# ifftshift of an 8192 x 8192 matrix: the order in which DMA packets walk the rows

## The chip, the cores and the metric

The kernel runs on one core of a Trainium2 chip. The metric is the device time of one execution in microseconds, median of several runs. Before the change it is 810.61 us (three runs, 810.15 to 810.87).

## The reference

```python
def setup_inputs():
    return {
        "x": np.random.randn(8192, 8192).astype(np.float32),
    }

def reference(x: np.ndarray) -> np.ndarray:
    return np.fft.ifftshift(x)
```

Both sides are even, so `ifftshift` moves every row by 4096 places and every column by 4096 places, around the end: `out[r, c] = x[(r + 4096) % 8192, (c + 4096) % 8192]`. The four quadrants change places diagonally. Nothing is computed; 268.4 MB (256 MiB) are read and as many are written.

## The kernel before

The kernel copies straight from the input in DRAM to the output in DRAM. No data comes into on-chip memory, and no compute engine has work. All DMAs are issued by SP (`nc.sync`), one after the other.

A row has 8192 floats, 32 KB; half a row, `hc`, is 16 KB, and a `piece` is half of that, 2048 floats or 8 KB. The function `both` (lines 25 to 34) issues one DMA for 64 rows (`rows = ENGINES * apart`, 16 x 4), and in each row for one piece of the left half and the same piece of the right half. The access pattern has three dimensions, outermost first: 64 rows with a step of one row, two halves with a step of half a row, 2048 contiguous floats. On the side of the input the halves go in the opposite order (step `-hc`) and the rows start 4096 further on, around the end. One DMA moves 64 x 2 x 8 KB = 1 MB.

The outermost dimension is split over the 16 DMA engines, so that each engine gets four neighbouring rows: engine e has rows 4e to 4e + 3 of the 64. Its eight packets of 8 KB are, in order, (row 0, left), (row 0, right), (row 1, left) and so on to (row 3, right). This order is not written in the loop; it follows from the access pattern.

The loops (lines 40 to 42) go over 128 blocks of 64 rows and, inside, over the two pieces of a half (`col`): 256 DMAs. Two successive DMAs thus finish a block of 64 rows, which is 2 MB of the input and 2 MB of the output, and the next two go on behind it.

The order of the work is that of the loops. The framework gives DMAs in turn one of eight semaphores, and from the ninth on each waits for the completion of the DMA eight places before it. So there are at most eight DMAs, 8 MB, in flight, and each DMA engine has up to eight DMAs' worth of packets queued.

Of the kernel before, what the change touches and what calls it, by code (L numbers as in the profile page):

```python
# [1 line left out]

# [4 lines left out]


ENGINES = 16  # L10


@with_exitstack
def kernel(
    ctx: ExitStack,
    tc: tile.TileContext,
    x: bass.AP,
    out: bass.AP,
):
    nc = tc.nc  # L20
    R, C = x.shape
    hr = R // 2
    hc = C // 2

    def both(queue, row, col, rows, piece):

        queue.dma_start(
            out=bass.AP(out.tensor, out.offset + row * C + col, [[C, rows], [hc, 2], [1, piece]]),
            in_=bass.AP(
                x.tensor,  # L30
                x.offset + (row + hr) % R * C + hc + col,
                [[C, rows], [-hc, 2], [1, piece]],
            ),
        )


    apart = 4
    piece = hc // 2
    rows = ENGINES * apart
    for row in range(0, R, rows):  # L40
        for col in (0, piece):
            both(nc.sync, row, col, rows, piece)


# [1 line left out]
_INS = ['x']  # L46
_OUTS = [((8192, 8192), 'float32')]


def kernel(**inputs):  # L50
    import numpy as _np
    import concourse.bacc as _bacc
    import concourse.tile as _tile
    from concourse import mybir as _mybir
    from concourse.bass_utils import run_bass_kernel_spmd as _run

    nc = _bacc.Bacc("TRN2", target_bir_lowering=False, num_devices=1)  # L57
    arrays, args = {}, []
    for name in _INS:
        a = _np.ascontiguousarray(inputs[name])  # L60
        if a.dtype.kind in "iu":
            a = a.astype(_np.int64)
        arrays[f"in_{name}_dram"] = a
        args.append(nc.dram_tensor(f"in_{name}_dram", a.shape, _mybir.dt.from_np(a.dtype), kind="ExternalInput").ap())
    for i, (shape, dtype) in enumerate(_OUTS):
        dt = _mybir.dt.from_np(_np.dtype(dtype))
        args.append(nc.dram_tensor(f"out_{i}_dram", shape, dt, kind="ExternalOutput").ap())
    with _tile.TileContext(nc) as tc:
        kernel(tc, *args)
    r = _run(nc, [arrays], core_ids=[0])  # L70
    got = tuple(r.results[0][f"out_{i}_dram"] for i in range(len(_OUTS)))
    return got[0]
```

## Time and profile before

| What | Value |
|---|---|
| median of the runs | 810.61 us |
| profiled execution, its own time | 810.44 us |
| its span, first to last instruction | 808.7 us |
| DMAs, size of each | 256, 1024 KB |
| packets on the DMA queue | 36864 |
| of these with data (8192 B) | 32768 |
| mean rate, one way | 332 GB/s |
| HBM read and written together | 664 GB/s over the span |
| median from issue to landing | 25.1 us |

The page shows only what an engine does for itself: here only four small constants that the framework writes with POOL, 0.2 us. What counts is the DMA part. The row "DMA" gives, in 40 equal slices of the span, the busy share of the 16 DMA engines in tenths; the row "GB/s" gives what they moved in each slice, one way (each byte is read and written once). "Busy" is from a packet's start to its end, whatever the packet waits for in between. The waits of SP's own queue ("SPq") tell whether the issuing of DMAs holds the DMA engines up. Line 27 is the `dma_start`, line 68 the end of the program.

The trace also has one record for each packet, with its start, its duration and its size, but without the engine's number; and the time of each of the 4096 completion signals, 16 for each DMA.

### The profile page before, as it was taken

What the parts mean: (1) busy time and instruction counts of PE and PEld (TensorE: products, weight loads), DVE (VectorE), ACT (ScalarE), POOL (GpSimd) and SP (SyncE); (2) the same over time, 40 slices, a digit from 0 to 9 for tenths busy, and PEclk for the clock granted to TensorE, in tenths of its full rate; (3) what the DMA queues carried; (4) which work ended last, traced back from release to release, by engine and by line L of the source; (5) the groups of instructions that cost most, each with busy time, mean ns of one, the idle gap of its engine ahead of it and who ended that gap; (6) DMA issues with size and microseconds to landing.
All of it is one profiled execution on the core that took longest, in us unless ns stands there. A gap on an engine that the chain in (4) does not pass through costs nothing. (4 is left out here: it accounts for less than half of the span.)

```text
span 808.7 us, 301 instructions
## 1 busy us (share of the span) xinstructions
POOL 0.2 (0%) x4
## 2 busy tenths in 40 slices
POOL 0000000000000000000000000000000000000000
DMA  8999999999999999999999999999999999999998
GB/s 301 331 335 329 336 334 330 335 332 336 332 335 334 336 331 334 339 328 335 331 335 339 334 334 337 331 336 330 336 334 331 339 332 334 333 336 331 337 335 294
DMA packets 36866, 268.47 MB, mean 332 GB/s; under 512 B 4096, under 2 KB 4096, under 8 KB 4096
## 3 DMA queue, kind: packets, MB, share of 16 engines
q1 hardware_dynamic: 36864, 268.45, 99.3%
q14 instruction: 2, 0.02, 0.0%
HBM read 268.44 MB, written 268.44 MB: 664 GB/s over the span
## 5 line engine op out<-in xcount | busy, mean ns | idle before, releaser
L57 POOL MEMSET const-bfloat16-1.0<- 128x1 bf16 x1 | 0.1, 102 | 0.0
L57 POOL MEMSET const-uint8-127<- 128x1 uint8 x1 | 0.1, 102 | 0.0
L57 POOL MEMSET const-float32-1.0<- 128x1 f32 x1 | 0.1, 99 | 0.0
L57 POOL MEMSET const-float32-0.0<- 128x1 f32 x1 | 0.1, 98 | 0.2 <-issue 0.2
## 6 DMA issues: line engine op xcount, KB each, us to landing
out_dram<-in_x_dram SPq DMA_DIRECT2D x256, 1024.0 KB, 25.1
```

Of the source, the lines that this page charges most:

```text
L57: nc = _bacc.Bacc("TRN2", target_bir_lowering=False, num_devices=1)
```

## The change

The number of DMAs (256), their size (1 MB), the packets' size (8 KB), the queue and the number of packets for each engine (eight) stay. What changes is which bytes make up a DMA, in which order an engine's packets go, and in which order the DMAs go.

A DMA now takes one piece (one quarter of a row: half `h`, piece `col` of it) of 128 rows, namely of every fourth row of a block of 512. The new pattern's outermost dimension has 16 entries, 4 rows apart, one for each engine; the second has `per` = 8 entries, 64 rows apart, which are the engine's eight packets. So engine e takes rows turn + 4e, turn + 4e + 64, turn + 4e + 128 and so on, with 64 rows (2 MB) from each packet to the next on both sides, and with the same columns. As the two halves are no longer in one DMA, the input's column is worked out for each DMA as `(col + hc) % C`.

The loops go, from the outside in, over the two pieces of a half (`col`), over the row modulo 4 (`turn`), over the 16 blocks of 512 rows, and over the two halves (`h`). For a given `col` and `turn` there are 32 DMAs, which walk through the whole matrix once; eight such passes make the run. The other half of the same rows follows in the next DMA, the next row 32 DMAs later, and the other piece of a half 128 DMAs later.

```diff
-    def both(queue, row, col, rows, piece):
-
+    def copy(queue, row, col, dims):
         queue.dma_start(
-            out=bass.AP(out.tensor, out.offset + row * C + col, [[C, rows], [hc, 2], [1, piece]]),
-            in_=bass.AP(
-                x.tensor,
-                x.offset + (row + hr) % R * C + hc + col,
-                [[C, rows], [-hc, 2], [1, piece]],
-            ),
+            out=bass.AP(out.tensor, out.offset + row * C + col, dims),
+            in_=bass.AP(x.tensor, x.offset + (row + hr) % R * C + (col + hc) % C, dims),
         )
 
 
     apart = 4
+    per = 8
     piece = hc // 2
-    rows = ENGINES * apart
-    for row in range(0, R, rows):
-        for col in (0, piece):
-            both(nc.sync, row, col, rows, piece)
+    step = ENGINES * apart
+    for col in (0, piece):
+        for turn in range(apart):
+            for block in range(0, R, step * per):
+                for h in (0, hc):
+                    copy(
+                        nc.sync,
+                        block + turn,
+                        h + col,
+                        [[apart * C, ENGINES], [step * C, per], [1, piece]],
+                    )
```

## The prediction

> **What bounds the kernel now.** I read the page first: how busy the DMA engines are, how many bytes go, and what a DMA takes from issue to landing.
>
> ```profile
> span 808.7 us, 301 instructions
> DMA  8999999999999999999999999999999999999998
> GB/s 301 331 335 329 336 334 330 335 332 336 332 335 334 336 331 334 339 328 335 331 335 339 334 334 337 331 336 330 336 334 331 339 332 334 333 336 331 337 335 294
> DMA packets 36866, 268.47 MB, mean 332 GB/s; under 512 B 4096, under 2 KB 4096, under 8 KB 4096
> q1 hardware_dynamic: 36864, 268.45, 99.3%
> HBM read 268.44 MB, written 268.44 MB: 664 GB/s over the span
> out_dram<-in_x_dram SPq DMA_DIRECT2D x256, 1024.0 KB, 25.1
> ```
>
> No compute engine works: this is 16 DMA engines, busy 99.3% of the span with 32768 packets of 8192 B (36864 less the 4096 small ones, which are the 16 completions of each of 256 DMAs). A packet counts as busy while it waits for memory, so 99.3% says that an engine is never without work, not that it runs as fast as it can.
>
> Next, whether the issuing queue holds anything up: its waits, and its line.
>
> ```profile
> SPq L27 <- DMA out_dram<-in_x_dram: 634.0, 248, 3.2
> SPq L68 <- DMA out_dram<-in_x_dram: 24.1, 4, 15.2
> L27 SPq DMA_DIRECT2D out_dram<-in_x_dram x256: 562/562/682, 0.7 to 783.1; - x128
> DMA to landing us min/median/max: 6.0/25.1/26.0
> ```
>
> An issue takes 0.562 us, and then SP waits 634.0 / 248 = 2.56 us for the DMA eight places back. The sum, 3.12 us, is the pace at which DMAs land; 25.1 us to landing is eight of them. SP follows, it does not lead.
>
> Then the rate by stretch of time.
>
> ```profile
> core 0: us, POOL busy (x), PEclk, DMA share, GB/s
> 2.00:6.00 4.00, 0.00 (x0) 1.00 0.95 338
> 6.00:13.00 7.00, 0.00 (x0) 1.00 1.01 349
> 13.00:20.00 7.00, 0.00 (x0) 1.00 0.99 311
> 20.00:100.00 80.00, 0.00 (x0) 1.00 1.00 333
> 100.00:400.00 300.00, 0.00 (x0) 1.00 1.00 334
> 400.00:780.00 380.00, 0.00 (x0) 1.00 1.00 334
> ```
>
> From 20 us to the end the rate stands at 333 to 334 GB/s each way; for 7 us early on it is 349. The engines are full in all of these, so the rate is set by how fast a packet of 8 KB goes through memory.
>
> Last, the trace's packet records one by one. The 32768 packets take 391.0 ns in the mean: 59.1% take at most 312 ns (309 in the mean) and the rest take 509 in the mean. 309 ns is the engine unhindered; the others meet something in memory. A packet's record begins 3 to 4 ns before the end of the one before it on its engine, so sequences of eight between two completions can be followed. For 3184 of the 4096 sequences that works without a doubt, and the mean by place in the sequence is
>
> ```
> place in the DMA   0     1     2     3     4     5     6     7
> written half       0     1     0     1     0     1     0     1   (row 0,0,1,1,2,2,3,3)
> mean ns          399.1 384.7 385.6 395.2 401.0 384.6 386.8 397.1   (each +-2.7; all 391.8)
> ```
>
> The landings also depend on address: the mean landing of a DMA follows that of the DMA before by 3.139 us on average, but by 3.088, 3.093, 3.138 and 3.235 us for DMAs 0, 1, 2 and 3 of every four. Two DMAs make a block of 64 rows (2 MB), so odd blocks cost (3.138 + 3.235) / 2 - (3.088 + 3.093) / 2 = 0.096 us a DMA more than even ones, 3%. Where the bytes lie moves the time by some per cent here, and the change moves nothing else.
>
> The span adds up: first DMA landed in the mean at 6.3 us, 255 x 3.139 = 800.4 more, 1.1 until the last engine's landing, 0.8 to close: 808.6 of 808.7. The profiled execution's own time is 810.44, 1.7 more than its span and 0.17 under the median of the runs, 810.61.
>
> **The change part by part.** 256 DMAs of 1 MB stay 256 of 1 MB, on the same queue, with eight 8 KB packets for each of 16 engines and the same eight in flight. The engines still start 4 rows (128 KB) apart. Both the reads (rows 4096 further, other half) and the writes are permuted in the same way. What differs is which packets follow each other.
>
> *Issue.* The pattern has dimensions 16 x 8 x 2048 in place of 64 x 2 x 2048. Cost between 0 and less than 0.562 us an instruction on SP, since the descriptor count is the same; I take 0. The cover is the 2.56 us of waiting behind every issue: an issue would have to grow from 0.56 to over 3.1 us before SP set the pace. Start (first DMA landed 6.0 us after issue at the earliest) and closing are the same work: 0.
>
> *Successive packets of an engine.* Before, an engine walks one patch of 4 rows, 128 KB: writes step 16 KB up, reads go 16 KB down and 48 KB up in turn. After, every packet is 64 rows, 2 MB, from the one before, on both sides; the other half of the row comes one DMA (3.1 us) later, the next quarter half a run later. No row of before is a 2 MB step inside a DMA. The nearest are places 0 and 4: at 0 the engine begins a new patch (2 MB on in every second DMA), at 4 it enters the second 64 KB of it. Their mean is (399.1 + 401.0) / 2 = 400.05 ns against 391.8 over all, +8.3 ns. With 2048 packets for each engine in the run that is 2048 x 8.3 = +17.0 us if every packet becomes such a one. From below: every packet like the cheapest place, 384.6, gives 2048 x -7.2 = -14.7 us; the early stretch's rate held throughout gives 800.4 x 334/349 - 800.4 = -34 us. From above: every packet like the hindered ones, 509 ns, 2048 x (509 - 391) = +242 us. I take +17.0, because it is the one price that belongs to stepping to a far place, which is what all packets do after.
>
> *The order of the DMAs.* Odd and even blocks of 64 rows now alternate inside each engine's eight packets, so the 0.096 us between them averages out: half of all DMAs lie in odd blocks before, half of every DMA's packets after; 0. If the odd blocks' cost came from meeting an even block's stragglers it would be paid more often: all at the odd price is +0.048 us a DMA, +12 us; all at the even price -12 us. Both lie inside the ends above.
>
> Here a rule of the Trainium skill speaks against the change. The row first: nothing in the trace of before has a run of steps at a large power of two on one engine, and its only 2 MB step, at place 0, costs 8 ns. The Trainium skill ("DMA: Bandwidth & Descriptors", section "Latency and other measured facts") lists copies between HBM tensors that fall from 214 GB/s to 164 at a row pitch of 2 MB and to 103 at 4 MB, and infers aliasing of lock-stepped streams. By an estimate from that page's 2 MB figure the 800 us would become 800 x 214/164 = 1044; no run here shows it yet.
>
> Sum: 810.44 + 17.0 = 827.4; against the median 827.6. I say 827.5.
>
> **The rivals.**
>
> *Faster: fixed low address bits keep the engines out of each other's way.* After, all packets in flight agree in quarter and in row modulo 4, and often in the half, and engine e stays at row 4e + turn of its 64 whatever packet it is at. Before, an engine that runs ahead sits on another row modulo 4 and another half. If hindered packets come from that mixing, they go: every packet like the cheapest place, 810.4 - 14.7 = 796; the early rate throughout, 776. For it: the early 349 GB/s falls in the first DMAs, when the 16 completions of one DMA lie about 0.7 to 1.1 us apart. Against it: that spread grows from 1.1 us to 2.4 over the run while the time of a DMA stays at 3.14 us, so running apart costs nothing that can be seen. It decides if the share of packets over 312 ns falls below 40.9%. The gain has an end nearby: the Trainium skill ("HBM Reference", section "Specifications") gives a pair's memory 716 GB/s, by which 536.9 MB take 750 us as an estimate; the trace's 664 GB/s over the span lies under it.
>
> *Same: memory is simply full.* If 664 GB/s is what mixed reads and writes get whatever the order, nothing changes: 809.0 to 812.2. For it: the flat 334 for 760 us. Against it: places and blocks differ by 3 to 4%, and the change replaces all these relations at once.
>
> *Much slower: steps of 2 MB collide.* If an engine's packets fall in the same part of memory one after the other, and engines that have run apart by a packet or more sit there too, then the hindered share grows. Each ten points of packets going from 309 to 509 ns cost 0.1 x 200 x 2048 = 41 us: 20 points give 892, all of them 1053. The Trainium skill's pitch rule above would land at this end. For it: the 3% between blocks shows that 2 MB steps matter to memory. Against it: place 0, the only 2 MB step now, costs 8 ns and not 100; and the engines' own distance, 128 KB, stays.
>
> **How the numbers follow.** The forecast, moderately slower by the price of the far step, 812 to 850: 0.42. Faster, 776 to 809: 0.37. Same: 0.06. Much slower, over 850: 0.15. The predicted time is that of the first, 827.5. What a measurement can tell from no change is about 0.2% (the runs spread over 0.09%), so faster 0.37, same 0.06, slower 0.42 + 0.15 = 0.57. Both signs have weight, so the range reaches into both: a quarter of the faster case, 0.09, lies under 788, and some 0.09 of the much slower one over 872, which leaves 0.18 out. The likeliest case's own range is 812 to 850.
>
> **What would show it.** Right: the same 36864 packets and 1024 KB a DMA; SP still waiting some 2.6 us behind each issue; the mean packet near 400 ns with no pattern by place, GB/s near 327 in every stretch, landings 3.2 us apart without a period of four. Wrong to the fast side: the share over 312 ns under 40%, GB/s near 340 or more throughout. Wrong to the slow side: that share over 50%, GB/s under 310, perhaps in some of the eight passes (quarter and turn) alone. An issue of over 3 us with the wait behind it gone would mean that SP has become the bound, which I leave out. A rate that differs between the two quarters or the four turns would mean that a fixed address bit carries a cost which before averages away in every DMA.

## The result and the profile after

The changed kernel takes 818.37 us (median of five runs, 818.13 to 818.46) against 810.78 us for the kernel before beside it (810.15 to 811.99): a ratio of 1.0087, 95% interval 1.0076 to 1.0098. It is slower by 7.6 us. The profiled execution took 818.4 us, 1.8 us over its span. Executions more than 1.5% above the fastest of their kernel (one with two blocks in a DMA, three with the first halves of other rows) count in the medians given below, but not in the ratios.

First the page of the changed kernel: its span, the DMA rows and the issues.

```profile
span 816.6 us, 301 instructions
GB/s 300 329 332 329 329 329 330 332 331 327 329 330 328 335 328 330 327 326 331 335 327 332 333 331 327 332 331 331 331 330 331 331 331 328 331 331 329 332 332 300
q1 hardware_dynamic: 36864, 268.45, 99.2%
HBM read 268.44 MB, written 268.44 MB: 657 GB/s over the span
out_dram<-in_x_dram SPq DMA_DIRECT2D x256, 1024.0 KB, 25.4
```

The work is the same, 36864 packets and 256 DMAs of 1 MB, and the engines are as full. The rate is lower in 33 of the 40 slices, mostly by a few GB/s: no stage has gone wrong, everything is a little slower.

Next SP's waits and its line; before, they had 634.0 us of waiting and 562 ns for an issue.

```profile
SPq L26 <- DMA out_dram<-in_x_dram: 639.6, 248, 3.1
L26 SPq DMA_DIRECT2D out_dram<-in_x_dram x256: 571/571/694, 0.7 to 790.9; - x128
```

An issue of the other pattern costs 9 ns more, and the wait behind it has grown too, to 2.58 us each. SP still follows.

Then the rate by stretches, with the same bounds as before.

```profile
20.00:100.00 80.00, 0.00 (x0) 1.00 1.00 330
100.00:400.00 300.00, 0.00 (x0) 1.00 1.00 330
400.00:780.00 380.00, 0.00 (x0) 1.00 1.00 331
```

330 to 331 GB/s where 333 to 334 stood. In the landings, the mean landing of a DMA follows that of the one before by 3.173 us instead of 3.139, which is 255 x 0.034 = +8.7 us; the last engine lands 0.6 us nearer to the mean of its DMA, and the first DMA 0.2 us earlier, so that +7.9 us remain, the difference of the spans. In the packet records the mean is 394.5 ns instead of 391.0, and 2048 x 3.5 = 7.3 us for each engine is nearly all of it. The share of packets over 312 ns rose from 40.9% to 47.8%, but those packets now take 488 ns in the mean instead of 509: more of them are hindered, each by less. That is no mark of every slower kernel, as the reads and writes below show.

### The profile page after: what moved, and what is told of

The parts are those of the page before. It is cut to its first block, busy times and chain, and to the rows that moved or that the text cites. A ratio compares the mean times of both kernels' runs of the same rounds, so it can differ in the third digit from the quotient of the medians.

```text
span 816.6 us, 301 instructions
## 1 busy us (share of the span) xinstructions
POOL 0.2 (0%) x4
## 2 busy tenths in 40 slices
DMA packets 36866, 268.47 MB, mean 329 GB/s; under 512 B 4096, under 2 KB 4096, under 8 KB 4096
## 3 DMA queue, kind: packets, MB, share of 16 engines
q1 hardware_dynamic: 36864, 268.45, 99.2%
```

## The experiments

What differs between the two kernels is which packet follows which. Five theories stood at one time or another:

- A, the prediction's: a 2 MB step from one packet of an engine to its next costs something by itself.
- B: the order of the DMAs (pieces and rows modulo 4 outermost) costs, since parts of a row go far apart in time.
- C: odd and even blocks of 64 rows mixed among the packets in flight cost.
- D: a packet is cheaper when a near one went just before on its engine; in its later form, when the *reads* of the two halves of one row, 16 KB apart, go one behind the other.
- E: both halves of rows must be among the packets in flight, whichever rows.

All comparisons are ratios to the kernel before, run in the same job. That matters: beside the experiments it took 810.9 to 811.4 us in four of the jobs and 821.5 us in the second. The order of an engine's packets is read from the access pattern; the trace shows no addresses. In code cuts, `...` stands for what is left out.

### Order of the DMAs, and what is in one

**The changed kernel's DMAs with the blocks outermost**

```diff
-    for col in (0, piece):
-        for turn in range(apart):
-            for block in range(0, R, step * per):
+    for block in range(0, R, step * per):
+        for turn in range(apart):
+            for col in (0, piece):
                 for h in (0, hc):
```

> The DMAs of the changed kernel, each unchanged, in another order: blocks of 512 rows outermost, then the row modulo 4, the piece and the half, so that all parts of a row go within 16 DMAs (50 us) of each other. Theory A (each 2 MB step of an engine costs about 7.6 us / 2048 = 3.7 ns): 818, as the changed kernel. Theory B (the parts of a row go too far apart in time, residues and pieces outermost): 811, as before. Theory C (odd and even blocks of 64 rows mixed among an engine's packets): 818.

Measured: 818.99 us, ratio 1.0096 (1.0083 to 1.0109). No gain from bringing the parts of a row together: B falls from the side of the change.

**Two blocks in a DMA**

```diff
-            out=bass.AP(..., [[C, rows], [hc, 2], [1, piece]]),
+            out=bass.AP(..., [[C, rows], [rows * C, 2], [1, piece]]),
...
-                [[C, rows], [-hc, 2], [1, piece]],
+                [[C, rows], [rows * C, 2], [1, piece]],
...
-    for row in range(0, R, rows):
+    for row in range(0, R, 2 * rows):
         for col in (0, piece):
-            both(nc.sync, row, col, rows, piece)
+            for h in (0, hc):
+                both(nc.sync, row, h + col, rows, piece)
```

> The kernel before with one step altered: a DMA takes four neighbouring rows for each engine as before, but the innermost pair of packets is the same quarter of the same row in two blocks of 64 rows, 2 MB apart, in place of the two halves of one row; the halves and pieces follow in the next three DMAs. Every step of an engine is about 2 MB, up or down, and odd and even blocks alternate, while the row modulo 4 varies inside the DMA as before and all parts of a row go within 4 DMAs. Theory A (2 MB steps): 818. Theory B (order of the DMAs): 811. Theory C (odd and even mixed): 818, with the packets in the odd block some 28 ns longer than those in the even one, as in the changed kernel.

Measured: 815.25 us, 1.0051 (1.0038 to 1.0064). Every step is far, but only about half of the loss is there. A, B and C each miss. The places in its trace didn't show C's 28 ns either: the means of the eight were 406, 403, 409, 372, 398, 383, 387 and 382 ns, falling along the DMA.

In its traced execution (814.25 us) this loss is of another kind than the change's. In the page,

```profile
span 812.5 us, 301 instructions
q1 hardware_dynamic: 36864, 268.45, 98.9%
```

the packets take 98.9% of 812.5, 803.6 us for each engine, against 99.3% of 808.7, 803.0 us, before; the mean packet of 8 KB is 391.3 ns against 391.0. Nearly all of the 3.8 us that the span has grown by lies between packets: from 20 to 780 us there are 12.3 us in which at most 13 of the 16 engines have a packet, 0.3 us before. The trace doesn't say why.

**The kernel before with the pieces outermost**

```diff
-    for row in range(0, R, rows):
-        for col in (0, piece):
+    for col in (0, piece):
+        for row in range(0, R, rows):
             both(nc.sync, row, col, rows, piece)
```

> The DMAs of the kernel before, each unchanged, with the loop over the two pieces of a half moved outermost: the second piece of each row goes half a run later. Theory A: 811, no step inside a DMA is altered. Theory B: between 812 and 818, as one of the two outer loops of the change is in it. Theory C: 811, though the odd blocks now come every second DMA in place of every second pair.

Measured: 810.95 us, 0.9997 (0.9989 to 1.0006). B falls from the side of the kernel before as well: half a run between the two pieces of a half costs nothing.

**One kind of block in a DMA**

```diff
-            for block in range(0, R, step * per):
-                for h in (0, hc):
...
-                        block + turn,
...
-                        [[apart * C, ENGINES], [step * C, per], [1, piece]],
+            for block in range(0, R, 2 * step * per):
+                for odd in (0, step):
+                    for h in (0, hc):
...
+                            block + odd + turn,
...
+                            [[apart * C, ENGINES], [2 * step * C, per], [1, piece]],
```

> The changed kernel with 128 rows (4 MB) in place of 64 (2 MB) between an engine's packets: a DMA covers only even or only odd blocks of 64 rows of 1024, two DMAs (the halves) of one kind and then two of the other. Engines 4 rows apart, residues and pieces outermost as in the change. Theory A: 818 or a little more, the steps are as far or farther. Theory B: 818, the outer order is the same. Theory C: 811, the mix is gone; DMAs of odd blocks would land some 3% later after their predecessor than those of even ones, as before the change.

Measured: 815.68 us, 1.0058 (1.0046 to 1.0070), 3.3 us under the first kernel of this job, which mixes the blocks. A predicted no gain from longer steps, C the whole gain; it was a third of the change's 0.87%, or two fifths beside the first kernel of this job. So how far the steps are, or which blocks mix, counts for something, and most of the loss is elsewhere.

### Reads or writes, near or far

**The pair 4 MB apart**

```diff
-                [[C, rows], [rows * C, 2], [1, piece]],
+                [[C, rows], [2 * rows * C, 2], [1, piece]],
```

(against the kernel with two blocks in a DMA; the same on both sides, and the loop takes 256 rows at a time)

> The kernel with two blocks in a DMA (815.3 against 811.05 for the kernel before beside it), its pair of packets now 128 rows, 4 MB, apart in place of 64, so that a DMA keeps to odd or to even blocks. Theory A (2 MB and longer steps cost by themselves): 815. Theory C (odd and even blocks mixed in flight): 811 to 812.5. Theory D (a packet is cheaper when its engine's neighbour in time lies within the same 128 KB, and the more so the nearer): 815. Theory E (the two halves of a row, bit 14 of the address, must both be in flight): 815.

Measured: 824.08 us beside 821.51, 1.0035 (1.0023 to 1.0048). Against 1.0051 for the pair 2 MB apart that is a small step in C's direction; the intervals overlap, and a loss remains.

**Two quarters of one half**

```diff
-            out=bass.AP(..., [[C, rows], [hc, 2], [1, piece]]),
+            out=bass.AP(..., [[C, rows], [-piece, 2], [1, piece]]),
...
-                [[C, rows], [-hc, 2], [1, piece]],
+                [[C, rows], [-piece, 2], [1, piece]],
...
     for row in range(0, R, rows):
-        for col in (0, piece):
-            both(nc.sync, row, col, rows, piece)
+        for h in (0, hc):
+            both(nc.sync, row, h + piece, rows, piece)
```

> The kernel before with the pair of packets being the two quarters of one half, 8 KB apart, in place of the same quarter of both halves; the other half follows in the next DMA. All steps are inside the patch of 4 rows. Theory A: 811, no far step. Theory C: 811, as before. Theory D: 811 or less, the steps are nearer. Theory E: 815, as the halves are no longer in one DMA.

Measured: 826.82 us, 1.0067 (1.0049 to 1.0086). No step inside a DMA leaves the engine's patch of 128 KB, the pairs are even nearer than before, 8 KB, and the loss is there. Far steps are not needed for it. A, C and the first form of D said 811 or less, that is 1.000; E alone said that it would lose, 815 or 1.005. What this kernel shares with the others that lose is that a row's two halves don't follow each other.

**Far writes**

```diff
+    out=bass.AP(..., [[C, rows], [rows * C, 2], [1, piece]]),    # pair of blocks
+    in_=bass.AP(..., [[C, rows], [-hc, 2], [1, piece]]),         # pair of halves
```

> Reads as in the kernel before (both halves of a row in a DMA), writes as in the kernel with two blocks in a DMA (same quarter of rows 2 MB apart). It moves the same bytes, but the blocks of 64 rows and the halves come out exchanged, so it is not an ifftshift. If the cost of the far pairs, 4.2 us, is paid on the write side: 815; on the read side: 811; on both: 813. Theory D allows any of these; under theory E the mix of halves is gone from the writes alone, 813.

Measured: 820.76 us, 0.9991 (0.9982 to 1.0001). In this diff and the next the steps stand as they come out; the code passes them as arguments.

**Far reads**

```diff
+    out=bass.AP(..., [[C, rows], [hc, 2], [1, piece]]),          # pair of halves
+    in_=bass.AP(..., [[C, rows], [rows * C, 2], [1, piece]]),    # pair of blocks
```

> Writes as in the kernel before, reads as in the kernel with two blocks in a DMA; the same exchange of blocks and halves in the output. Cost on the read side: 815; on the write side: 811; on both: 813.

Measured: 826.46 us, 1.0064 (1.0051 to 1.0076). The pair of halves matters to the reads; the writes may go 2 MB apart for nothing. This gave D its later form. The rates of the two kernels, on one chip, far writes first:

```profile
100.00:400.00 300.00, 0.00 (x0) 1.00 1.00 331
400.00:780.00 380.00, 0.00 (x0) 1.00 1.00 330
...
100.00:400.00 300.00, 0.00 (x0) 1.00 1.00 327
400.00:780.00 380.00, 0.00 (x0) 1.00 1.00 328
```

Here the loss is in the packets: 399.4 ns in the mean with far reads, 394.5 with far writes. But fewer of them are over 312 ns, 39.0% instead of 40.3%, and those take 541 ns instead of 521; the two quarters have 37.9% and 543. In the changed kernel it was the other way, so the share of hindered packets doesn't tell whether a kernel is slower.

### Same row, or only both halves

**Halves of other rows**

```diff
+            pair(nc.sync, row, col, rows * C + hc, rows * C - hc, rows, piece)
+            pair(nc.sync, row, hc + col, rows * C - hc, rows * C + hc, rows, piece)
```

(`pair` is `both` with the step of the pair given for the output and for the input)

> As ratios to the kernel before in the same job, since that kernel took 811.05 us beside the first four runs and 821.51 beside the next four. The pair of packets is the right half of a row and the left half of the row 64 further (on the read side), so both halves are in flight in every DMA as before, but the two packets are 2 MB apart and not of one row. Theory E (both halves have to be among the reads in flight, whichever row): 1.000. Theory D, now for reads alone and for the two halves of the same row, 16 KB apart, going one behind the other: 1.004 to 1.007, as the two kernels whose reads had no such neighbour (1.0051 and 1.0064).

Measured: 873.66 us; the ratio, from the runs of 864 to 867 us, is 1.0674 (1.0657 to 1.0691), outside all theories. The page's DMA rows, the waits and SP's line of this kernel say why, and that it is none of them:

```profile
DMA  8899989989798979899999989888999989989988
q1 hardware_dynamic: 36864, 268.45, 90.4%
out_dram<-in_x_dram SPq DMA_DIRECT2D x256, 1024.0 KB, 8.5
...
SPq L26 <- DMA out_dram<-in_x_dram: 687.4, 128, 10.3
...
L26 SPq EVENT_SEMAPHORE  x124: 17/17/17, 24.8 to 854.9; - x124
```

The engines are busy 90.4% instead of 99.2%, a DMA lands 8.5 us after its issue instead of 25, and SP has 124 instructions that only wait. The two DMAs of a group of rows interleave in the output. The framework, as it seems, took them for overlapping and made a DMA wait for a recent one; its reason isn't on record, the waits are. With fewer DMAs in flight the engines ran dry.

**The same pairs without those waits**

```diff
-    for row in range(0, R, 2 * rows):
-        for col in (0, piece):
-            pair(nc.sync, row, col, rows * C + hc, rows * C - hc, rows, piece)
-            pair(nc.sync, row, hc + col, rows * C - hc, rows * C + hc, rows, piece)
+    for h in (0, 1):
+        bend = hc - 2 * h * hc
+        for row in range(0, R, 2 * rows):
+            for col in (0, piece):
+                pair(nc.sync, row, h * hc + col, rows * C + bend, rows * C - bend, rows, piece)
```

> The pairs of the earlier kernel with halves of other rows (right half of a row, left half of the row 64 further, on the read side), in an order in which no DMA waits for a recent one: all pairs of this kind first, then all of the other kind. So 25 us from issue to landing, as before the change. Theory E (strict alternation of the halves, whatever the rows): 1.000. Theory D (the same row): 1.004 to 1.008, as the other kernels of this DMA size without the pairs on the read side.

Measured: 816.57 us, 1.0062 (1.0041 to 1.0083). The same rows of its page and of its waits:

```profile
q1 hardware_dynamic: 36864, 268.45, 99.2%
out_dram<-in_x_dram SPq DMA_DIRECT2D x256, 1024.0 KB, 25.4
...
SPq L26 <- DMA out_dram<-in_x_dram: 638.6, 248, 3.4
```

The DMAs are the same and only their order differs, so the other 6% were the waits. What is left says E is wrong: right and left halves of rows alternate strictly, but of different rows, and the loss is like that of the far reads (1.0064).

**Halves on two queues**

```diff
-                        nc.sync,
+                        nc.scalar if h else nc.sync,
```

> The changed kernel's DMAs with the right halves issued by ACT and the left ones by SP, so that the DMA engines have both in hand at once: each engine takes packets of both queues in turn. Theories D and E: 1.000 to 1.003, since the two halves of a row are again next to each other in time. Theory A (2 MB steps as such): 1.009, as the changed kernel, or more.

Measured: 818.31 us, 1.0078 (1.0057 to 1.0098). Both D and E missed. For D the packet records give a reason: SP's queue runs ahead of ACT's by 0.7 of a DMA all through (3.18 DMAs' packets begun against 2.46 at 20 us, 126.2 against 125.5 at 800 us), so that about six packets of each queue, by that estimate a dozen in all, go between the two halves of a row. The queues brought the halves into flight together, but by that estimate not one behind the other. One of the six runs took 812.93 us, the others 817.44 to 818.84; whether the queues went in step in it isn't known, since another was traced.

**The changed kernel again**

> The changed kernel as it is, to have its ratio on the same chip as its neighbours here: 1.0087 if the ratio doesn't depend on the chip, whatever the time of the kernel before.

Measured: 818.19 us, 1.0087 (1.0074 to 1.0100), the kernel without any edit, in another job than at first. It holds to the digit.

**The halves in the opposite order**

```diff
-            out=bass.AP(out.tensor, out.offset + row * C + col, [[C, rows], [hc, 2], [1, piece]]),
+            out=bass.AP(out.tensor, out.offset + row * C + hc + col, [[C, rows], [-hc, 2], [1, piece]]),
...
-                x.offset + (row + hr) % R * C + hc + col,
-                [[C, rows], [-hc, 2], [1, piece]],
+                x.offset + (row + hr) % R * C + col,
+                [[C, rows], [hc, 2], [1, piece]],
```

> The kernel before with the two halves in the opposite order: reads go 16 KB up and the writes 16 KB down within a row, and 48 KB up on. Theories D and E: 1.000, since the pairs are the same. If it is the direction of the read pair that counts, another time, on either side.

Measured: 811.01 us, 1.0000 (0.9991 to 1.0008). Which half is read first doesn't matter.

### The same DMAs, other neighbours

The kernels so far changed the pair and the steps together. The next four have DMAs of 256 KB, two packets for each engine, so that the order of the loops alone decides what follows what. The first two share one function:

```diff
+    def halves(queue, row, col):
+        queue.dma_start(
+            out=bass.AP(..., [[apart * C, ENGINES], [hc, 2], [1, piece]]),
+            in_=bass.AP(..., [[apart * C, ENGINES], [-hc, 2], [1, piece]]),
+        )
```

**Near pairs** (`for block` of 64 rows, `for col`, `for turn`: the order of the kernel before)

> The packet order of the kernel before, in DMAs a quarter as large: 256 KB, for each engine the two halves of one row; then the next of the engine's four rows, then the other piece, then the next 64 rows. It is the base for the other three; 12288 completions more cost, by their 9 ns in the trace over 16 engines, about 7 us, so about 1.009 to the kernel before if eight DMAs of 256 KB in flight are enough. Its issues, 1024 x 0.56 us = 577 us, fit. All theories the same.

**Far pairs** (`for col`, `for turn`, `for block`: the next DMA is 2 MB on)

> The same DMAs as the near pairs, each unchanged, in another order: the next DMA is 64 rows (2 MB) further, pieces and rows modulo 4 outermost as in the change. Every second step of an engine is 2 MB, the others go to the other half of the same row. Theory D: as the near pairs, within 0.1%. Theory A: half of the change's cost, 0.4% over the near pairs.

**The changed order** (the changed kernel's `copy` with `per = 2`; four DMAs down the rows for one half, then four for the other)

> The packet order of the changed kernel in DMAs of 256 KB: two packets 2 MB apart, four such DMAs in a row for one half and then four for the other, so that the two halves of a row are eight packets apart on their engine. Theories A and D both: 0.9% over the near pairs.

**Halves two packets apart** (the same DMAs, `for h` innermost)

> The same DMAs as in the changed order, with the halves alternating innermost: a row's two halves are two packets (0.8 us) apart on their engine, with a packet 2 MB away between them. Theory A: 0.9% over the near pairs. Theory D: less than that, and near zero if what one half leaves behind in memory lasts for a packet.

Measured, all in one job:

| Order of an engine's packets | us | ratio to before (95%) | over near pairs |
|---|---|---|---|
| near pairs | 812.24 | 1.0014 (1.0005 to 1.0023) | |
| far pairs | 814.05 | 1.0036 (1.0022 to 1.0050) | 0.22% |
| halves two apart, far | 818.55 | 1.0095 (1.0081 to 1.0108) | 0.81% |
| changed order, halves eight apart | 820.60 | 1.0119 (1.0106 to 1.0133) | 1.05% |

The rate by stretches shows the same without the ends of the run. Near pairs, 20 us to 780 us (the columns end with DMA share and GB/s):

```profile
20.00:100.00 80.00, 0.00 (x0) 1.00 1.00 333
100.00:400.00 300.00, 0.00 (x0) 1.00 1.01 332
400.00:780.00 380.00, 0.00 (x0) 1.00 1.00 333
```

Far pairs:

```profile
20.00:100.00 80.00, 0.00 (x0) 1.00 1.00 333
100.00:400.00 300.00, 0.00 (x0) 1.00 1.00 333
400.00:780.00 380.00, 0.00 (x0) 1.00 1.00 333
```

The changed order:

```profile
20.00:100.00 80.00, 0.00 (x0) 1.00 1.00 329
100.00:400.00 300.00, 0.00 (x0) 1.00 1.00 330
400.00:780.00 380.00, 0.00 (x0) 1.00 1.00 330
```

Half of the far pairs' steps are 2 MB, and the rate of the near pairs is there; take the pairs away and the rate of the changed kernel is there. Of the 8.4 us between the first and the last row of the table, 6.6, nearly four fifths, come back when the two halves follow each other, though the steps between the pairs stay far. With a foreign packet between the halves most of that is lost again: 4.5 us of the 6.6. For D this is what it said in kind; it said within 0.1% for the far pairs, and 0.22% were measured. Whether the far steps have that price is at the edge of what can be told: the two intervals just touch, and the profiled executions lie the other way, with spans of 811.6 us for near pairs and 811.0 for far ones. A's half way would have been 0.5% by this job's own figures. The cost of small DMAs, estimated at 0.9%, was 0.14%.

Two limits of this table. The changed order has twice the far steps of the far pairs; at 1.8 us for each 1024 of them they would make 3.6 of the 8.4 us, and the pairs 4.8. And by the pages' DMA shares (99.6% of 811.6 us for near pairs, 99.0% of 819.1 us for the changed order) the packets themselves take 2.6 us more, while the other 4.9 us of the profiled difference lie between packets. So the table shows what the order costs, not that each packet becomes that much slower.

**Pieces of 4 KB**

```diff
-    piece = hc // 2
+    piece = hc // 4
...
-        for col in (0, piece):
+        for col in range(0, hc, piece):
```

> The kernel before with pieces of 4 KB in place of 8 KB: pairs of halves as before, still 16 KB apart, but half as far apart in time; DMAs of 512 KB, twice as many packets. If the gain from a pair is one of time, it grows: 0.995 to 1.000 in spite of 4096 more completions (2.3 us, 0.3%). If a pair is worth what it is however close, and a packet of 4 KB costs a little more than half of one of 8 KB: 1.003 and more.

Measured: 831.72 us, 1.0261 (1.0242 to 1.0280). Two packets of 4 KB take 2 x 204 ns for what one packet of 8 KB takes 391 ns for; even the commonest duration, 159 ns, is more than half of 309. In the first 100 us it ran well under its later 329 GB/s, as the first slices of its page and the stretch from 20 us on show:

```profile
GB/s 248 295 300 308 320 334 331 324 328 336 322 333 329 332 323 326 327 331 332 325 332 330 327 327 332 333 328 327 337 317 329 327 332 332 329 332 328 329 330 277
...
20.00:100.00 80.00, 0.00 (x0) 1.00 1.03 307
100.00:400.00 300.00, 0.00 (x0) 1.00 1.03 329
```

That start was not followed up. Halves closer in time gain nothing that outweighs this. No version was found that beats both kernels: the far writes at 0.9991 have an interval that holds no change, and they are no `ifftshift`.

## Why the prediction was right or wrong

*What bounds the kernel, and the parts costed at nothing.* Right. The issue grew by 9 ns and stayed covered by a wait of 2.58 us; start and end moved by 0.2 and 0.6 us. Nearly the whole change is in how long packets take.

*Successive packets of an engine, +17.0 us.* The direction came out as forecast, the term was more than twice too large (7.3 us by the packets, 7.6 by the medians), and its reason was mostly the wrong one; that the sign was right is largely luck. The step that failed is the price: +8.3 ns, read from places 0 and 4 of the DMA as the price of "stepping to a far place". Two things were wrong with it. A far step costs much less: the far pairs take 1.8 us for 1024 far steps of an engine, 1.8 ns each, and two quarters of one half lose 0.67% without one inside a DMA. And the means by place were no price of a step. Place 4 is no far place: its read goes 48 KB up, as at places 2 and 6, which stood at 385.6 and 386.8 ns in the prediction's own table, while places 3 and 7, reached by 16 KB like 1 and 5, stood at 395.2 and 397.1, above the mean. Two kernels with the same pairs, pieces outermost and opposite order, have places 0 and 4 above the mean again, by 6 and 12 ns together, but 3 and 7 too, by 13 and 12 (from the sequences that can be followed without a doubt, some 1650 of 4096 in each). So the pattern is there, and isn't that of the steps. In the changed kernel's profile the eight places, alike in their steps but for the first, stand at 381, 408, 380, 411, 383, 415, 380 and 404 ns; in the same kernel's profile in the later job at 392, 391, 396, 394, 400, 401, 396 and 394, at the same ratio. A pattern that goes while the time stays doesn't price anything. The prediction named the event that does cost, the other half of the row coming a DMA later, as part of the same bullet, but put the price on the step.

*What stands in its place.* In the kernel before, the reads of a row's two halves, 16 KB apart, go one behind the other on an engine. Every kernel that keeps this on the read side with DMAs of 1 MB lies between 0.9991 and 1.0000 (pieces outermost, opposite order, far writes); every one that gives it up lies between 1.0035 and 1.0096, with near steps or far ones (the one slowed by added waits left aside). That giving up the relation costs most of the loss is shown, by the far reads beside the far writes and by the two quarters above all. Why two such reads go faster, and why 8 KB apart doesn't do it, is not: the trace has no view of what happens inside memory. Other near distances, such as the same piece of neighbouring rows, 32 KB apart, were not run, so whether it must be the two halves of a row is open. Between none and some two fifths of the loss may be that of the far steps, by the table of the small DMAs; the two kernels with 4 MB steps were 0.2 and 0.3 to 0.4% better than theirs with 2 MB, so either the distance or the mix of odd and even blocks has a part in that. That split stays open.

One rival is left in some of the experiments. In five kernels (two blocks in a DMA, 4 MB apart, two quarters, far writes, halves of other rows) there are 5 to 13 us, between 20 and 780 us, in which at most 13 engines have a packet. It can't be what costs in general: the far writes have 7.9 us of it and lose nothing, and the far reads and the changed kernel lose with under 0.5 us. For two blocks in a DMA it may be the whole loss.

*The order of the DMAs, 0.* Right for the outer loops. The period of four DMAs went as foretold: the correlation of a landing interval with the fourth after it fell from 0.51 to 0.12.

*Rival "faster".* What it leaned on came about: the engines stay together, with the first and last completion of a DMA 1.1 us apart at the end as at the start, where the kernel before had grown to 2.4 us. It gained nothing, as its counter-argument had it: the rate stayed at 330 GB/s, not the early 349. The share over 312 ns, which had to fall below 40.9%, rose.

*Rival "same".* Close in size, but 0.87% is far outside 0.2%. The order counts; the outer order of the DMAs alone (0.9997 with the pieces outermost) doesn't.

*Rival "much slower".* It needed 2 MB steps to collide. They hardly do: 330 GB/s, where an engine's steps inside a DMA are nothing else. The Trainium skill's figures for large row pitches ("DMA: Bandwidth & Descriptors", section "Latency and other measured facts") would have given 1044 us by the estimate in the prediction. The measurement decides: 818 us. Here the engines stood 128 KB apart, by the access pattern, and only an engine's own next packet was 2 MB away; to such steps the figures don't carry over in this kernel.

## What to carry to other kernels

Where DMAs alone bound a kernel, ask of each engine's packet sequence what its next read is, not only how large the packets are or how the outer loops run: here the pairing of reads 16 KB apart was worth most of 0.9%, and the outer order of the DMAs nothing. A mean by place is no price of a step until all places that the same step leads to agree, in a second run too. And before explaining a slow variant by memory, look at its time from issue to landing and at the engines' share: here a fall from 25 us to 8.5 went with waits between DMAs, and a share of 98.9% with packets no slower than before.

## What the runs showed that was not expected

Beside the experiments the same kernel took 810.9 to 811.4 us on four chips and 821.5 us on a fifth, 1.3% more, which is above the whole effect studied; ratios were therefore compared, and the changed kernel's was 1.0087 in both jobs that it ran in.

Reads and writes answer to different things: with the pairs taken from the reads alone (they then go 2 MB apart) the ratio was 1.0064, from the writes alone 0.9991.

A DMA of 256 KB, with eight in flight, cost only 0.14% over one of 1 MB, with SP waiting 162.7 us in all instead of 634.0; packets of 4 KB cost 2.6%.
